# Weight sums moved into the SSD stage, and a fifth feed-forward pair begun early, in a decoder layer's kernel

## The chip, the cores and the metric

The kernel runs on one core of one Trainium2 chip. The metric is the device time of one execution in microseconds (us); for the kernel before there are three runs, of which the median counts. The profile and the trace come from one more execution, which has a time of its own. Engines are called as the profile calls them: PE (TensorE matmuls), PEld (TensorE's weight loads), DVE (VectorE), ACT (ScalarE), POOL (GpSimd), SP (SyncE, which here issues the DMAs).

## The reference

One layer of a decoder trunk on 1024 tokens and 16 meta tokens, width 1024, all in float32. What matters here:

```
proj = h @ w_in          # q_lat, kv_lat, k_pe, z, xbc, dt_raw, g_attn, g_ssd
y_attn = mla_branch(q_lat, kv_lat, k_pe, ...)        # attention over latents
y_ssd  = ssd_branch(z, xbc, dt_raw, ...)             # Mamba-2 SSD mixer, 4 groups
mixed  = sigmoid(g_attn) * y_attn + sigmoid(g_ssd) * y_ssd
h = layer_norm(DEEPNORM_ALPHA * h + mixed @ w_out)
u = causal_dwconv(h @ w_up)                          # 2 x 2816 columns, width 3
gate, val = split(u)
ffn = (silu(gate) * val) @ w_down
h = layer_norm(DEEPNORM_ALPHA * h + ffn)
```

## The kernel before

Every product in float32 is made of three passes of matmuls: each operand is split into a high part (rounded by ACT) and a low part (source minus high part, on DVE), and high times high, low times high and high times low are summed. `split` (lines 198 to 200) does it for one tile, `load_w` (143 to 164) for a weight that comes by DMA, `mm3` (166) and `mm3h` (184, matmuls at line 191) multiply.

The program has stages, which overlap a little at their borders: the first norm and the latents, attention by heads (to about 540 us of the trace), the gates stage (540 to 740), the SSD stage (740 to 1420), the output projections by two halves of the tokens with the middle norm (1420 to 1750), the feed-forward up stage (1750 to 2227), the down stage and the last norm (to 2475).

**Gates stage** (loop at 778 to 788). Eight turns m of `gate` and `o_proj` matmuls. Between them are set `dt_chain` (701: step sizes of the SSD, mostly DVE; its transposes on PE, line 736, wait for the copy of line 733), `h_centered` (751: its matmul, line 762, waits for DVE's sums of line 760) and `down_sums` (738). `down_sums(j)`, called for j = 0 to 10, loads two 512 KB blocks of the down weight, makes four differences of 128 x 512 on DVE (lines 744 to 747) and stores both blocks again; the down stage reads them 1500 us later.

**SSD stage** (loop at 867). Four groups g, in each the B and C parts and four tiles ti: a convolution (`conv`, 799), the chunk work, and the z gate, whose last DVE operation is the multiply of line 951. Each tile has two weights of 512 KB through `load_w`, which has two raw buffers. The 16 row sums `wm` of the output weight (line 1018, DVE), which the projections need, stand in the code behind this stage, but run when their buffers in pool Dr are free.

**Up stage** (line 1084 on). The up projection is a Strassen-Winograd product by halves: for each of 22 pairs f of column blocks seven products (numbers 1 to 7) of 24 matmuls instead of eight. `wload` reads the blocks, POOL makes four weight sums s1 to s4 (lines 1108 to 1111), and `wsplit` splits what the products take. The right operands ("forms") are made from the two halves of the normed tokens: B1 of the first half, T1 to T4 and B2 once the second half's norm is known. Products 1 and 2 need B1 alone. So `NHEAD` = 4 pairs are "begun": `top(f)` and `second(f)` make their products 1 and 2 while the norm's root is taken and the forms are made. In the loop (1213 to 1255) a begun pair then has five products left, a whole pair all seven. `first(f)` (1140) sets up a pair: for a begun one its product 6 into the PSUM pair x0 and the addition u2 = p1 + x0 on DVE (line 1148). Product 5 overwrites x0, so it waits for that addition.

A scheduler sets the order of the instructions on each engine from priorities and dependences; `issue_after` ties one instruction behind another. Each engine, and SP's queue of DMA issues, works in order.

Of the kernel before, what the change touches and what calls it, by code (L numbers as in the profile page):

```python
# [103 lines left out]
def tile_hybrid(ctx: ExitStack, tc: tile.TileContext, x, vecs, consts, cos, sin, win, wqb, wk, wv,  # L104
# [156 lines left out]
    gv_d = [dtile(f"gv_d{k}", [P, SEQ]) for k in range(NFF)]  # L261
    t13_d = [dtile(f"t13_d{k}", [P, D]) for k in range(KH)]
# [413 lines left out]
    with pool("B3", 1) as p3:  # L676
# [61 lines left out]
        def down_sums(j):  # L738

            x, y = (p3.tile([P, D], F32, name=k, tag=k) for k in ("tw1", "tw2"))  # L740
            nc.sync.dma_start(x, wdl[j])
            nc.sync.dma_start(y, wdl[j + KH])
            (b11, b12), (b21, b22) = ((t[:, :512], t[:, 512:]) for t in (x, y))
            nc.vector.tensor_sub(b11, b12, b11)
            nc.vector.tensor_sub(b12, b22, b12)
            nc.vector.tensor_sub(b22, b22, b11)
            nc.vector.tensor_sub(b21, b21, b22)
            nc.sync.dma_start(t13_d[j], x)
            nc.sync.dma_start(t42_d[j], y)

# [27 lines left out]
        for m in range(KT):  # L778
# [18 lines left out]
    with pool("C", 1) as p:  # L797
# [36 lines left out]
        def norm_factors(g, ssq):  # L834

            for b in range(3):
# [4 lines left out]
                nc.sync.dma_start(rr_d[g][:, lo(b):C1[b]], r[:, off:n])  # L841

        ngs = 0
        late = None
        for g in range(GROUPS):
# [21 lines left out]
            for i in range(4):  # L867
# [11 lines left out]
                for b in range(3):  # L879
# [71 lines left out]
                    nc.vector.tensor_mul(y[:, off:n], y[:, off:n], tz[:, off:n])  # L951
# [26 lines left out]
    p = eD.enter_context(pool("Dr", 1, "right"))  # L978
# [57 lines left out]
    for hi in range(2):  # L1036
# [136 lines left out]
    with tc.issue_after(root_end[0]):  # L1173
        second(0)
# [344 lines left out]
```

## Time and profile before

| what | us |
|---|---|
| runs, median (lowest to highest) | 2478.08 (2471.75 to 2480.24) |
| the profiled execution's own time | 2476.96 |
| its span in the trace | 2474.9 |
| PE busy in the span | 2379.6 (96%) |
| DVE busy | 1746.3 (71%) |
| ACT busy | 1137.5 (46%) |
| POOL busy | 202.2 (8%) |

The span is the time from the first to the last instruction of the trace. A share is an average over stages with different limits. The mean granted TensorE clock of this execution was 0.986 of full speed.

### The profile page before, as it was taken

The numbers are of one execution on the slowest core, as the hardware profiler recorded it, in microseconds if no ns is written. First come the engines' busy times: TensorE is split into PE (matmuls) and PEld (weight loads), VectorE is DVE, ScalarE is ACT, GpSimd is POOL, SyncE is SP. The second block draws the span as 40 slices with busy tenths as digits, with TensorE's granted clock in tenths as the row PEclk, the third lists the DMA queues.
The fourth block names the chain that finished last, engine by engine and source line by source line (L and its number), as shares of the span: only waits on it lengthen the run. The fifth ranks groups of instructions, "written<-read, shape, count | busy, mean of one in ns | idle before, by whom it ended". The sixth has DMA issues, their size and how long they took to land.

```text
span 2474.9 us, 42581 instructions
## 1 busy us (share of the span) xinstructions
PE 2379.6 (96%) x16319; PEld 2252.3 (91%) x16319; DVE 1746.3 (71%) x3945; ACT 1137.5 (46%) x2481; POOL 202.2 (8%) x190
## 2 busy tenths in 40 slices
PE   6999999999999999999999999999789999999996
PEld 5998988989999999999999999999789999998885
DVE  6467667676767678776877744855778777766858
ACT  5335545562226555445554432432544444445443
POOL 0000000000000000000000000202332222210004
PEclk9999999999999999999999999999899999999998
DMA  6120110147792312222212254644322222229332
GB/s 205 47 66 29 42 38 26 46 137 254 246 308 85 101 64 87 82 79 89 84 64 82 66 176 139 212 154 148 116 86 81 83 83 81 78 85 304 123 111 98
DMA packets 124620, 277.29 MB, mean 112 GB/s; under 512 B 14720, under 2 KB 49792, under 8 KB 122368
## 3 DMA queue, kind: packets, MB, share of 16 engines
q1 hardware_dynamic: 124416, 274.57, 33.8%
q8 instruction: 128, 2.10, 0.3%
q14 instruction: 76, 0.62, 0.1%
HBM read 209.62 MB, written 62.80 MB: 110 GB/s over the span
## 4 chain that ended last, share of the span: by engine, by line
PE 80%; DVE 8%; DMA 6%; issue 2%; ACT 2%; POOL 1%; SPq 0%; DVEq 0%; ACTq 0%; POOLq 0%
PE d L191 25%; PE g L171 11%; PE g L173 11%; PE g L172 11%; PE g L1339 5%; PE c L617 3%; PE c L1339 2%; PE c L908 2%; PE c L611 1%; PE c L932 1%; PE c L912 1%; DMA yl<-y_d 1%; DMA tw<-wdl 1%; DMA wraw<-wup 1%; DVE wl L161 1%
## 5 line engine op out<-in xcount | busy, mean ns | idle before, releaser
L191 PE MATMUL d<-f,wh 128*128 128x258 f32 (+1 forms) x4000 | 655.5, 286 | 28.2 <-DVE u L1148 15.7
L191 PEld LDWEIGHTS d<-f,wh 128*128 128x128 f32 x4000 | 558.7, 192 | 31.0 <-ACT wh L199 20.0
L171 PE MATMUL g<-h,wh 128*128 128x348 f32 (+3 forms) x1560 | 508.0, 326 | 4.7 <-ACT lat L399 4.7
L172 PE MATMUL g<-h,wl 128*128 128x348 f32 (+3 forms) x1560 | 507.4, 325 | 0.0
L173 PE MATMUL g<-h,wh 128*128 128x348 f32 (+3 forms) x1560 | 507.0, 325 | 0.0
L191 PE MATMUL d<-f,wl 128*128 128x258 f32 (+1 forms) x2000 | 407.6, 285 | 6.1 <-DVE wl L200 4.3
L191 PEld LDWEIGHTS d<-f,wl 128*128 128x128 f32 x2000 | 314.4, 192 | 7.9 <-DVE wl L200 5.5
L171 PEld LDWEIGHTS g<-h,wh 128*128 128x128 f32 x1560 | 295.4, 189 | 7.4 <-ACT lat L399 5.0
L172 PEld LDWEIGHTS g<-h,wl 128*128 128x128 f32 x1560 | 295.8, 190 | 2.7 <-issue 2.7
L173 PEld LDWEIGHTS g<-h,wh 128*128 128x128 f32 x1560 | 295.1, 189 | 2.7 <-issue 2.7
L161 DVE TENSOR_TENSOR wl<-wraw,wh 128x512 fp32r<-128x512 f32 (+2 forms) x278 | 193.6, 698 | 142.1 <-ACT wh L160 138.9
L160 ACT CAST wh<-wraw 128x512 fp32r<-128x512 f32 (+2 forms) x278 | 167.1, 604 | 254.8 <-PE d L191 122.6
L171 PE MATMUL g<-a,wh 128*128 128x348 f32 (+2 forms) x456 | 149.2, 328 | 1.9 <-DVE kn L200 1.1
L172 PE MATMUL g<-a,wl 128*128 128x348 f32 (+2 forms) x456 | 148.1, 325 | 0.0
L173 PE MATMUL g<-a,wh 128*128 128x348 f32 (+2 forms) x456 | 147.8, 324 | 0.0
L200 DVE TENSOR_TENSOR wl<-wraw,wh 128x512 fp32r<-128x512 f32 x136 | 99.6, 741 | 60.3 <-ACT wh L199 60.2
L199 ACT CAST wh<-wraw 128x512 fp32r<-128x512 f32 x136 | 82.7, 617 | 106.5 <-DMA wraw<-wup 48.9
L813 DVE SCALAR_TENSOR_TENSOR xc<-g,V,xc 128x347 f32<-128x347 f32 (+2 forms) x180 | 103.5, 576 | 33.0 <-ACT xc L809 30.2
L898 ACT ACTIVATE G<-ac,tok 116x116 f32<-116x116 f32 x288 | 91.6, 379 | 42.5 <-PE c L908 42.5
L1339 PE MATMUL g<-wh,dh 128*128 128x512 f32 x352 | 110.7, 396 | 0.0
L1133 DVE SCALAR_TENSOR_TENSOR va<-u,V,va 128x512 f32<-128x512 f32 x88 | 94.8, 1077 | 20.4 <-ACT va L1131 19.1
L199 ACT CAST wh<-s 128x512 fp32r<-128x512 f32 x88 | 53.9, 617 | 88.2 <-PE d L191 45.6
(306 smaller groups left out, 4216.0 us busy)
## 6 DMA issues: line engine op xcount, KB each, us to landing
wraw<-win SPq DMA_DIRECT2D x65, 512.0 KB, 3.4
wraw<-wup SPq DMA_DIRECT2D x48, 512.0 KB, 3.4
ac<-cs_d SPq DMA_DIRECT2D x16, 1044.0 KB, 5.7
wraw<-wos SPq DMA_DIRECT2D x32, 512.0 KB, 3.9
tw<-wdl SPq DMA_DIRECT2D x22, 512.0 KB, 4.6
t_d<-tw SPq DMA_DIRECT2D x22, 512.0 KB, 3.1
gv<-gv_d SPq DMA_DIRECT2D x44, 256.0 KB, 5.9
wraw<-t_d SPq DMA_DIRECT2D x44, 256.0 KB, 3.4
```

The lines of the kernel that those rows point to most:

```text
L160: nc.scalar.copy(h[:, :n * ncol], r)
L161: nc.vector.tensor_sub(l[:, :n * ncol], r, f32(h[:, :n * ncol]))
L171: nc.tensor.matmul(ps, ah, bh, start=(k == 0), stop=False)
L172: nc.tensor.matmul(ps, al, bh, start=False, stop=False)
L173: nc.tensor.matmul(ps, ah, bl, start=False, stop=(k == n - 1))
L191: ins = nc.tensor.matmul(ps[:, PO + c0:PO + c1], a, b[:, c0:c1], start=(start and k == 0 and i == 0), stop=(k == n - 1 and i == 2), skip_g ...
L199: nc.scalar.copy(H, src)
L200: nc.vector.tensor_sub(L, src, f32(H))
L813: nc.vector.scalar_tensor_tensor(t[:, l:n], ps[:, hal + l - s:hal + n - s], vec("cw", (3 - s) * 24 + ct), t[:, l:n], ALU.mult, ALU.add)
L898: nc.scalar.activation(G_[:, k * S:(k + 1) * S], ac[:S, hh, C0[b] + k * S:C0[b] + (k + 1) * S], AF.Relu, bias=tok[:, 3 * b + k, 32 + hd:33 ...
L1133: nc.vector.scalar_tensor_tensor(t, src[:, 2 - k:HN - k], vec("fw", (2 - k) * 44 + ti), t, ALU.mult, ALU.add)
L1339: nc.tensor.matmul(pss[t], a[:, o], b, start=(first and j == 0 and i == 0), stop=(j == KH - 1 and i == 2), skip_group_check=not first)
```

## The change

The sums `down_sums` leave the gates stage. They are made in the SSD stage, after the tiles ti = 1 to 11, from a pool "DS" of their own with two buffers of each kind, and their first subtraction is tied behind the last multiply of the tile. Pool Dr is divided (into `prr`, Dt and others). Five pairs are begun instead of four: the fifth, pair 4, is begun first, and its two partial results lie in DRAM until its turn. In the loop begun and whole pairs take turns: 0, 5, 4, 6, 1, 7, 2, 8, 3, 9, then 10 to 21. `prod` ties each product behind the one before it, so that PE keeps the order of the program. The norm's forms are made in the order T2, T3, T1, then `first(0)`, then B2 and T4; the four subtractions for T4 (b21) go from POOL to DVE, ahead of `first(0)`. No product is added or left out.

```diff
-            for j in range(2 * m - 2, 2 * m):
-                if 0 <= j < KH:
-                    down_sums(j)
...
+    with pool("DS", 2, "right") as pds, pool("C", 1) as p:
...
+        def down_sums(j, after):
+            x, y = (pds.tile([P, D], F32, name=k, tag=k) for k in ("tw1", "tw2"))
+            nc.sync.dma_start(x, wdl[j])
+            nc.sync.dma_start(y, wdl[j + KH])
+            (b11, b12), (b21, b22) = ((t[:, :512], t[:, 512:]) for t in (x, y))
+            with tc.issue_after(after):
+                nc.vector.tensor_sub(b11, b12, b11)
+                nc.vector.tensor_sub(b12, b22, b12)
+                nc.vector.tensor_sub(b22, b22, b11)
+                nc.vector.tensor_sub(b21, b21, b22)
+            nc.sync.dma_start(t13_d[j], x)
+            nc.sync.dma_start(t42_d[j], y)
...
-                    nc.vector.tensor_mul(y[:, off:n], y[:, off:n], tz[:, off:n])
+                    ins = nc.vector.tensor_mul(y[:, off:n], y[:, off:n], tz[:, off:n])
...
+                if 0 < ti <= KH:
+                    down_sums(ti - 1, ins.ins)
...
     def prod(ps, q, w, start=True):
-        return mm3h(ps, w[q], rhs[q], start)
+        with tc.issue_after(order[0]) if order else ExitStack():
+            ins = mm3h(ps, w[q], rhs[q], start)
+        order[:] = [ins.ins]
+        return ins
...
     def first(f):
...
-        if f < NHEAD:
+        if f < NHEAD + NMORE:
+            if f >= NHEAD:
+                for k in ("p1", "c11"):
+                    q[k] = etile(k, NHEAD)
+                    nc.sync.dma_start(q[k], hx_d[f - NHEAD][k])
             prod(q["x0"], 6, q["w"])
...
     def second(f):
...
+        if f >= NHEAD:
+            for k in ("p1", "c11"):
+                nc.sync.dma_start(hx_d[f - NHEAD][k], st[f][k])
...
+    heads = [*range(NHEAD, NHEAD + NMORE), *range(NHEAD)]
...
+    for j in range(hB):
+        b21.append(ftile(prr, F32))
+        nc.sync.dma_start(b21[j], h1_d[j + hB][:, cols(0)])
     for j in range(hB):
         T1[j] = form(pf2, b11[j])
     for j in range(hB):
+        nc.vector.tensor_sub(b21[j], b21[j], t2[j])
+    rhs.update({5: T1, 6: T2, 7: T3})
...
+    first(0)
+    for j in range(hB):
         B2[j] = form(pf2, rs[j + hB])
     for j in range(hB):
-        b21 = dtmp("b21", "r", 8)
-        nc.sync.dma_start(b21, h1_d[j + hB][:, cols(0)])
-        nc.gpsimd.tensor_sub(b21, b21, t2[j])
-        T4[j] = form(pf2, b21)
-    rhs.update({3: B2, 4: T4, 5: T1, 6: T2, 7: T3})
+        T4[j] = form(pf2, b21[j])
+    rhs.update({3: B2, 4: T4})
...
-    first(0)
-    begun = 1
-    for f in range(NFF):
+    turns = [f for pr in itertools.zip_longest([0, NHEAD, *range(1, NHEAD)], range(NHEAD + NMORE, NFF)) for f in pr
+             if f is not None]
+    for f, nxt in zip(turns, turns[1:] + [None]):
         q = st[f]
-        while begun < min(NHEAD, f + 2):
-            first(begun)
-            begun += 1
...
-        while begun < min(NFF, f + (3 if f + 1 < NHEAD else 2)):
-            first(begun)
-            begun += 1
+        if nxt:
+            first(nxt)
         prod(x0, 3, w, False)
```

**DVE, the sums of one block.** Before, they stand in the gates stage among the `dt_chain` (lines 715 to 724); tw1 and tw2 are the two blocks:

```order
L744 TENSOR_TENSOR tw1_7807<-tw1_7807 128x512
L745 TENSOR_TENSOR tw1_7807<-tw2_7808,tw1_7807 128x512
L746 TENSOR_TENSOR tw2_7808<-tw2_7808,tw1_7807 128x512
L723 TENSOR_SCALAR xx_8018<-xx_8018 64x348
L747 TENSOR_TENSOR tw2_7808<-tw2_7808 128x512
L715 TENSOR_SCALAR w_8021<-u_8020 64x348
L716 RECIPROCAL w_8021<-w_8021 64x348
L161 TENSOR_TENSOR wl_7622<-wraw_7619,wh_7621 128x512
```

Now they stand at the end of an SSD tile, here ti = 6, by turns with the next tile's convolution (line 800, tile xc):

```order
L952 TENSOR_TENSOR y_12369<-y_12369,tz_12400 128x344
L837 TENSOR_TENSOR tw1_12407<-tw1_12407 128x512
L800 SCALAR_TENSOR_TENSOR xc_12452<-g_12427,V_72,xc_12452 128x347
L959 TENSOR_TENSOR ssq_11480<-ssq_11480,tz_12400 128x344
L838 TENSOR_TENSOR tw1_12407<-tw2_12408,tw1_12407 128x512
L800 SCALAR_TENSOR_TENSOR xc_12452<-g_12427,V_72,xc_12452 128x346
L839 TENSOR_TENSOR tw2_12408<-tw2_12408,tw1_12407 128x512
L800 SCALAR_TENSOR_TENSOR xc_12452<-g_12427,V_72,xc_12452 128x345
L840 TENSOR_TENSOR tw2_12408<-tw2_12408 128x512
L804 SCALAR_TENSOR_TENSOR xc_12452<-th_12457,xc_12452 128x348
```

In the same move the 16 row sums wm went from the place between the gates and the SSD stage to group 3, behind the sums of tile ti = 11, because their buffers lie where pool DS lies.

**SP, the DMA issues at the end of the same tile.** Before, with the stores of y, the next weights (wraw) and the decay rows (ac):

```order
L952 DMA y_d6_172<-y_12261 128x334
L952 DMA y_d6_172<-y_12345 128x348
L147 DMA wraw_12940<-win 128x1024
L952 DMA y_d6_172<-y_12424 128x344
L147 DMA wraw_13086<-win 128x1024
L873 DMA ac_13574<-cs_d_188 128x2088
```

Now:

```order
L953 DMA y_d6_174<-y_12206 128x334
L953 DMA y_d6_174<-y_12290 128x348
L149 DMA wraw_12905<-win 128x1024
L953 DMA y_d6_174<-y_12369 128x344
L841 DMA t13_d5_129<-tw1_12407 128x1024
L842 DMA t42_d5_140<-tw2_12408 128x1024
L833 DMA tw1_13419<-wdl 128x1024
L834 DMA tw2_13420<-wdl 128x1024
L149 DMA wraw_13051<-win 128x1024
L874 DMA ac_13549<-cs_d_190 128x2088
```

Two stores and two loads stand ahead of the next weight load; the loads take the buffers that those of an earlier block free.

**PE, the start of the feed-forward loop.** Before, d_21039 is x0 of pair 0, wh_21027 a weight of product 6 and wh_21031 one of product 5; the last four rows of product 6 and the first four of product 5:

```order
L191 MATMUL d_21039<-f_20918,wl_21028 128x258
L191 MATMUL d_21039<-f_20918,wl_21028 128x256
L191 MATMUL d_21039<-f_20919,wh_21027 128x258
L191 MATMUL d_21039<-f_20919,wh_21027 128x256
L191 MATMUL d_21039<-f_20942,wh_21031 128x258
L191 MATMUL d_21039<-f_20942,wh_21031 128x256
L191 MATMUL d_21039<-f_20942,wl_21032 128x258
L191 MATMUL d_21039<-f_20942,wl_21032 128x256
```

Now, with d_21081 as x0, wh_21069 for product 6, and d_21144 (x2), wh_21065 for product 7:

```order
L193 MATMUL d_21081<-f_20992,wl_21070 128x258
L193 MATMUL d_21081<-f_20992,wl_21070 128x256
L193 MATMUL d_21081<-f_20993,wh_21069 128x258
L193 MATMUL d_21081<-f_20993,wh_21069 128x256
L193 MATMUL d_21144<-f_20997,wh_21065 128x258
L193 MATMUL d_21144<-f_20997,wh_21065 128x256
L193 MATMUL d_21144<-f_20997,wl_21066 128x258
L193 MATMUL d_21144<-f_20997,wl_21066 128x256
```

Product 7, into another PSUM pair, now stands between products 6 and 5.

**DVE at the same place.** Before, the low parts (line 200) of the last T1 form, of B2 (r) and T4 (b21) stand ahead of the addition u2, line 1148:

```order
L200 TENSOR_TENSOR f_20955<-f_20868,f_20954 128x514
L200 TENSOR_TENSOR f_20959<-r_20364,f_20958 128x514
L200 TENSOR_TENSOR f_20963<-r_20431,f_20962 128x514
L200 TENSOR_TENSOR f_20967<-r_20498,f_20966 128x514
L200 TENSOR_TENSOR f_20971<-r_20565,f_20970 128x514
L200 TENSOR_TENSOR f_20978<-b21_20974,f_20977 128x514
L200 TENSOR_TENSOR f_20985<-b21_20981,f_20984 128x514
L200 TENSOR_TENSOR f_20992<-b21_20988,f_20991 128x514
L200 TENSOR_TENSOR f_20999<-b21_20995,f_20998 128x514
L1148 TENSOR_TENSOR u2_21064<-p1_20618,d_21039 128x514
L200 TENSOR_TENSOR wl_21020<-wraw_21009,wh_21019 128x512
L200 TENSOR_TENSOR wl_21032<-s1_21011,wh_21031 128x512
```

Now the subtractions of line 1225 (b21), a weight of pair 5 (s3_21211), the last T1 form and one B2 form stand ahead of it (line 1164):

```order
L1225 TENSOR_TENSOR f_21018<-f_21018,t2_20964 128x514
L202 TENSOR_TENSOR f_21033<-f_20940,f_21032 128x514
L202 TENSOR_TENSOR wl_21230<-s3_21211,wh_21229 128x512
L202 TENSOR_TENSOR f_21037<-f_20942,f_21036 128x514
L1225 TENSOR_TENSOR f_21020<-f_21020,t2_20977 128x514
L1225 TENSOR_TENSOR f_21022<-f_21022,t2_20990 128x514
L202 TENSOR_TENSOR f_21109<-f_20373,f_21108 128x514
L1164 TENSOR_TENSOR u2_21106<-p1_20670,d_21081 128x514
L202 TENSOR_TENSOR wl_21074<-s1_21053,wh_21073 128x512
L202 TENSOR_TENSOR wl_21078<-s4_21056,wh_21077 128x512
L202 TENSOR_TENSOR f_21113<-f_20440,f_21112 128x514
L202 TENSOR_TENSOR f_21117<-f_20507,f_21116 128x514
```

Of the forms behind T1, three B2 forms and all of T4 now stand behind the addition. From the fourth T2 form to the addition DVE has 22 instructions in the new order.

## Rows read from the trace of the kernel before

**Rows 1.** The page's part 1: busy us, share of the span, instructions of each engine.

```profile
PE 2379.6 (96%) x16319; PEld 2252.3 (91%) x16319; DVE 1746.3 (71%) x3945; ACT 1137.5 (46%) x2481; POOL 202.2 (8%) x190
```

**Rows 2.** Windows, up stage: us, busy of PE, PEld, DVE, ACT, POOL; clock, DMA, GB/s.

```profile
1910.00:2210.00 300.00, 300.00 (x2487) 300.00 (x2486) 228.92 (x297) 146.37 (x238) 77.20 (x56) 1.00 0.25 82
1770.00:1870.00 100.00, 72.06 (x535) 69.00 (x535) 81.59 (x105) 45.49 (x73) 42.97 (x27) 0.88 0.25 82
1770.00:1800.00 30.00, 13.25 (x81) 12.10 (x80) 25.05 (x33) 18.09 (x30) 15.92 (x9) 0.66 0.25 80
1790.00:1800.00 10.00, 5.68 (x24) 5.27 (x24) 7.41 (x10) 6.24 (x9) 3.81 (x4) 0.51 0.18 53
```

**Rows 3.** Waits of PE, whole span: line, releaser, us in all, times, longest.

```profile
PE d L191 <- DVE u L1148: 15.7, 1, 15.7
...
PE c L736 <- DVE q L733: 3.6, 2, 3.4
...
PE c L762 <- DVE hs L760: 2.1, 1, 2.1
```

**Rows 4.** Timeline of PE, 1755 to 1795 us: start, length, line, tiles, shapes, count, [idle before].

```profile
1755.24 1.35 PE L227 MATMUL d<-K,ir 128*128 128x128 f32 x10
...
1777.73 0.50 PE L191 MATMUL d<-f,wh 128*128 128x258 f32 x2 [0.42 <-DVE f L200]
...
1793.97 0.77 PE L191 MATMUL d<-f,wh 128*128 128x258 f32 x2 [15.73 <-DVE u L1148]
```

**Rows 5.** Timeline of DVE, 1770 to 1795 us.

```profile
1771.15 4.08 DVE L200 TENSOR_TENSOR wl<-s,wh 128x512 fp32r<-128x512 f32 x3
...
1776.99 0.69 DVE L200 TENSOR_TENSOR f<-t,f 128x514 fp32r<-128x514 f32 x1
...
1783.63 2.50 DVE L200 TENSOR_TENSOR f<-r,f 128x514 fp32r<-128x514 f32 x4
```

**Rows 6.** Timeline of POOL, 1765 to 1795 us.

```profile
1767.26 1.50 POOL L1108 TENSOR_TENSOR s<-wraw 128x512 f32<-128x512 f32 x1 [32.95 <-DMA wraw<-wup]
...
1772.24 1.61 POOL L1111 TENSOR_TENSOR s<-wraw,s 128x512 f32<-128x512 f32 x1
1781.67 10.18 POOL L1205 TENSOR_TENSOR b<-b,t 128x514 f32<-128x514 f32 x4 [7.81 <-DMA b<-h_d]
```

**Rows 7.** The page's part 6, DMA issues: transfer, count, KB each, median us to landing.

```profile
wraw<-wup SPq DMA_DIRECT2D x48, 512.0 KB, 3.4
...
t_d<-tw SPq DMA_DIRECT2D x22, 512.0 KB, 3.1
```

**Rows 8.** Windows, gates stage, same columns as rows 2.

```profile
620.00:660.00 40.00, 36.42 (x214) 35.21 (x214) 30.78 (x62) 9.36 (x21) 0.00 (x0) 0.91 0.64 223
680.00:700.00 20.00, 20.00 (x129) 20.00 (x128) 10.11 (x20) 4.01 (x8) 0.00 (x0) 1.00 0.98 326
700.00:720.00 20.00, 17.94 (x104) 17.22 (x103) 13.46 (x27) 4.24 (x9) 0.30 (x3) 0.91 0.83 268
```

**Rows 9.** Groups of DVE, 540 to 740 us: busy, mean ns, idle before and releaser.

```profile
L1018 DVE TENSOR_REDUCE wm<-wr 128x1 f32<-128x512 f32 x12 | 7.9, 681 | 3.3 <-DMA wr<-wor 3.3
L744 DVE TENSOR_TENSOR tw<-tw 128x512 f32<-128x512 f32 x11 | 7.6, 689 | 9.0 <-DMA tw<-wdl 9.0
```

**Rows 10.** Windows, SSD stage: about one tile, and a stretch of group 3.

```profile
848.00:880.00 32.00, 31.73 (x222) 29.64 (x221) 25.81 (x65) 19.00 (x48) 0.13 (x2) 1.00 0.29 92
1240.00:1280.00 40.00, 40.00 (x270) 39.05 (x269) 28.86 (x60) 18.13 (x37) 0.10 (x1) 1.00 0.13 43
```

**Rows 11.** Timeline of SP's queue, 866 to 900 us: y stores and weight loads.

```profile
867.00 0.32 SPq L952 DMA_DIRECT2D y_d<-y  x1
875.10 0.33 SPq L147 DMA_DIRECT2D wraw<-win  x1
...
892.71 0.33 SPq L147 DMA_DIRECT2D wraw<-win  x1
898.88 0.32 SPq L952 DMA_DIRECT2D y_d<-y  x1
```

More of the change, by code (lines that the diff above doesn't have):

```diff
@@ L1 @@
+import itertools
 from contextlib import ExitStack
@@ L90 @@
 NHEAD = 4
+NMORE = 1
 KH = NFF // 2
@@ L261, in tile_hybrid @@
     gv_d = [dtile(f"gv_d{k}", [P, SEQ]) for k in range(NFF)]
+    hx_d = [{k: dtile(f"hx_{k}{j}", [P, HN]) for k in ("p1", "c11")} for j in range(NMORE)]
     t13_d = [dtile(f"t13_d{k}", [P, D]) for k in range(KH)]
@@ L737, in dt_chain @@
                 nc.scalar.copy(tok[:, 3 * c:3 * c + 3, :], tp[:S, :192].rearrange("p (a b) -> p a b", b=64))
[L738 to L749, printed above, removed]
         def h_centered(c):
@@ L796, in tile_hybrid @@
     NB = 348
-    with pool("C", 1) as p:
+    with pool("DS", 2, "right") as pds, pool("C", 1) as p:
         def conv(blk, ct, tag, bufs):
@@ L977, in tile_hybrid @@
     eD = ctx.enter_context(ExitStack())
-    p = eD.enter_context(pool("Dr", 1, "right"))
+    prr = eD.enter_context(pool("Dr", 8, "right"))
+    eT = ctx.enter_context(ExitStack())
+    p = eT.enter_context(pool("Dt", 1, "right"))
     eM = ctx.enter_context(ExitStack())
@@ L1115, in wrest @@
             for q, a in ((4, a22), (7, s3), (6, s2), (5, s1), (3, s4)):
-                r[q] = wsplit(p0, a, 4) if q in (7, 6, 3) else wsplit(pe[0], a, 3)
+                r[q] = wsplit(p0, a, 4) if q in (4, 7, 6) else wsplit(pe[0], a, 3)
             return r
+    order = []
     def prod(ps, q, w, start=True):
-        return mm3h(ps, w[q], rhs[q], start)
+        with tc.issue_after(order[0]) if order else ExitStack():
+            ins = mm3h(ps, w[q], rhs[q], start)
+        order[:] = [ins.ins]
+        return ins
     pe = []
     def etile(name, bufs):
-        return (p0 if name in ("p1", "c11") else pe[0]).tile([P, HN], F32, name=name, tag=name, bufs=bufs)
+        pl = p0 if name in ("p1", "c11") else pe[0] if name in ("u2", "u4") else pe[1]
+        return pl.tile([P, HN], F32, name=name, tag=name, bufs=bufs)
     def conv_up(src, ti, tag, bufs):
@@ L1169, in top @@
         return ins
-    rd = inv_root(ssq, HN, 1.0 / D, LN_EPS, top(0), lambda: top(1))
+    heads = [*range(NHEAD, NHEAD + NMORE), *range(NHEAD)]
+    rd = inv_root(ssq, HN, 1.0 / D, LN_EPS, top(heads[0]), lambda: top(heads[1]))
     with tc.issue_after(root_end[0]):
-        second(0)
-    second(1)
-    for f in range(2, NHEAD, 2):
-        top(f)
-        top(f + 1)
-        second(f)
-        second(f + 1)
+        second(heads[0])
+    second(heads[1])
+    for i in range(2, len(heads), 2):
+        for f in heads[i:i + 2]:
+            top(f)
+        for f in heads[i:i + 2]:
+            second(f)
     T1, T2, T3, T4, B2 = ([None] * hB for _ in range(5))
@@ L1197, in tile_hybrid @@
         T3[j] = form(pf2, rs[j])
+    b21 = []
+    for j in range(hB):
+        b21.append(ftile(prr, F32))
+        nc.sync.dma_start(b21[j], h1_d[j + hB][:, cols(0)])
     for j in range(hB):
@@ L1220, in tile_hybrid @@
         prod(x2, 7, w)
-        if f < NHEAD:
+        if f < NHEAD + NMORE:
             c11, u2 = q["c11"], q["u2"]
@@ L1233, in tile_hybrid @@
         u4 = etile("u4", 2)
-        if f < NHEAD:
+        if f < NHEAD + NMORE:
             nc.vector.tensor_add(u4, p1, half(x0))
```

16 lines of the change are left out of this document (9 added, 7 removed).

## The prediction

> **What bounds the kernel now.** I read the share of each engine first, then the waits of PE, then windows, and only for one place the timelines. PE is busy for 96% of the span and no other engine for more than 71% [rows 1]; the change neither adds nor drops a product, so it can only win back time in which PE idles or runs at the lower of its two clock levels (1.2 instead of 2.4 GHz; the profile's clock column is 1.00 at the higher). A measurement of this kernel can tell 0.3% from no change, 7.4 us.
>
> The rate to measure by: in the steady part of the up stage 2487 matmuls fill 300 us without a gap [rows 2], 0.1206 us each. A product of 24 is 2.9 us, a whole pair of seven 20.2 us, the five products of a begun pair 14.5 us.
>
> Two places lose time that the change touches. The large one is the passage into the up stage: in 1770 to 1870 PE is busy for 72.06 us of 100 [rows 2], so 27.9 us are idle, and in 1790 to 1800 the clock is 0.51, 24 matmuls take 5.68 us where the rate gives 2.9, which is 2.8 more. Loss 30.7 us. (By counts, 535 matmuls at 0.1206 are 64.5 us, loss 35.5; some records can be missing, so I keep the lower.) The reader is to see that half of it is one wait: PE sat 15.73 us until the addition u2 of line 1148 was done [rows 3, 4]. On PE product 5 of pair 0 stood directly behind product 6, whose sum that addition reads and whose PSUM product 5 overwrites. On DVE the addition stood behind the forms, and the last of these behind POOL, whose four b21 subtractions ran from 1781.67 for 10.18 us [rows 6]. What is left, 12 us of idle, is spread over four begun pairs in a row, each with few matmuls to hide its weights.
>
> The small one is the gates stage: 3.6 us of idle for the dt transposes and 2.1 for the centering matmul [rows 3], both waits for DVE, in stretches with a clock of 0.91 [rows 8].
>
> **The change part by part.** *Start of the up stage.* After the root (PE's row at 1755.24, done by 1756.6) come eight products instead of six ahead of product 6, because a fifth pair is begun: 8 x 2.9 = 23.2, to 1779.8 [rows 4]. Product 6's weights: POOL's first sum began at 1767.26, the fourth at 1772.24 [rows 6], so three sums take 5.0. In the new order one more top weight comes first; I take its split as done at about 1769.6, the load behind it 3.4 [rows 7], so 1773.0, sums to 1778.0, rounding and split about two DVE operations of 0.63 each plus lock (below) 0.8: 1780.1. PE idles 0.3 us here. Products 6 and 7 run to 1785.9.
>
> The addition u2: the fourth T2 form began at 1776.99 and ended 0.6 later, behind three weight splits that took 4.08 [rows 5]; these move behind it and one more top split, 0.6, comes ahead, so 1777.6 - 4.08 + 0.6 = 1774.1. From there DVE has 22 instructions, of which the trace has the price 2.50/4 = 0.63 each [rows 5]: 13.9. Five POOL sums (four of pair 0, one of pair 5) fall into this time. How much each slows DVE the trace bounds from both sides: the four forms at 1783.63 ran at 0.63 each while POOL subtracted, nothing lost; the three splits at 1771.15 took 4.08 instead of 1.9, with 2.7 us of POOL's work beside them, so 2.2/2.7 of POOL's time, 1.3 us a sum. I take 1.0, nearer the second, since those were sums of the same kind: 5.0. The addition ends at 1774.1 + 13.9 + 5.0 = 1793.0. PE, free at 1785.9, waits 7.1 us where it waited 15.7. I keep one product at the lower clock, +2.8, as the trace shows it after such a wait.
>
> The rule that speaks against this step is in the Trainium skill, "SBUF — State Buffer", section "SBUF: two separate sides": a VectorE operation with two SBUF inputs and a GpSimd operation that reads SBUF shut each other out for the whole instruction. Taken in full for VectorE, with a sum at 5.0/3 = 1.65 us [rows 6], five sums cost 8.3 instead of 5.0, product 5 starts 3.3 us later, and the sum below becomes 2459. The splits at 1771.15 lie near that rule; the forms at 1783.63 lost nothing, and there POOL's subtractions took 2.5 us each, as if POOL had been the one shut out.
>
> The remaining weight waits, 12 us over four begun pairs in a row, fall as whole pairs stand between them: DVE and POOL then have 34.7 us of PE for two pairs instead of 29. I take 3 us for all five (none to 12). Loss after 0.3 + 7.1 + 2.8 + 3 = 13; the gain is 30.7 - 13 = 18 (bounds 9, when the weight waits stay at 12, and 28, when the addition comes in time). The spill of pair 4, two stores and two loads of 263 KB, costs nothing: its loads are issued a whole pair (20 us) ahead of their use and a load of 512 KB lands in 3.4 [rows 7]; without that cover one load, 3.4. The b21 subtractions on DVE are 4 of the 22.
>
> *Gates stage.* Without the sums DVE sheds 44 x 0.689 = 30 us and waits for their loads (9.0 us before line 744 alone [rows 9]), which held up what was queued behind. The transposes and the centering matmul need the same DVE results with a shorter queue. Idle 5.7, and a lower clock behind it: against 129 matmuls per 20 us [rows 8], 620 to 660 has 44 fewer and 700 to 720 has 25 fewer, 69 x 0.155 = 10.7 us in all. I take 7 (bounds 3 and 10.7): the chain of dt is long on DVE even alone.
>
> *SSD stage.* Each of eleven tiles gets four subtractions, 2.74 us by line 744 [rows 9], 30 in all; a tile of 31.9 us (stores at 867.00 and 898.88 [rows 11]) has 6.2 us of idle DVE [rows 10]. They fit, but not at any moment: they stand between the next convolution's operations, which free PSUM for PE. The 16 row sums, 10.9 us, go where DVE has 11.1 us idle in 40 [rows 9, 10]. On SP two stores that wait for the sums, and two loads that wait until an older store has landed (3.1 us [rows 7]), now stand ahead of the next weight load. That load is late by some 2.7 + 3.1 = 6 us; weight loads are 17.6 us apart [rows 11] and need 3.4, so it is hidden. DMA is at 0.29 there, and 2 MB more per tile are 66 GB/s beside 92 [rows 10]; the gates stage moved 326 [rows 8]. Bounds 0 and 30.2 + 10.9 = 41, all of it on the path; I take 4, near the lower end, because PE is busy for 31.73 of 32 us there with DVE idle for a fifth.
>
> **Sum.** 2476.96 (the profiled execution, 1.1 below the median of the runs) - 18 - 7 + 4 = **2456 us**.
>
> **The rivals.**
> 1. *The addition is nearly as late* (lock in full, weight waits stay), gain 10, and the gates stage gives back 5, since dt's own chain on DVE stays: 2477 - 10 - 5 + 4 = 2466. For it: splits at 1.36 us instead of 0.63 beside POOL. Against: the long POOL subtractions are gone.
> 2. *Almost all comes back*: the addition in time, gain 28, gates 7, SSD free: 2442. For it: 6.2 us of idle DVE in each tile. Against: 22 instructions and five sums from 1774 end 7 us too late by the sum above.
> 3. *No change*: the gain at the start is 9, and of the 41 us a third, 14, comes up in the SSD stage and eats the 7 of the gates: 2475. The sums would then merely have changed their place.
> 4. *Slower*: in each SSD tile the subtractions hold up the next convolution's operations on DVE, so PSUM comes free late and PE waits: 41 against 25, 2493. It decides from 25/11 = 2.3 us a tile on, most of the 2.74. For it: the sums stand between those of line 800, and SP's weight load behind them. Against: idle DVE and the slack of that load.
> That the change doesn't do what it says is ruled out by the order: product 7 stands between 6 and 5, and the sums behind the tiles.
>
> **How the numbers follow.** Forecast 0.58, rival 1 0.18, rival 2 0.14, rivals 3 and 4 0.05 each. The first three are all below 2470.6, over 0.3% faster: 0.90. Rival 3 is the same, 0.05, rival 4 slower, 0.05. The range goes from 2438 (28 and 10.7 won, nothing paid) to 2470 (rival 1 with the SSD stage at twice its price): it leaves out rivals 3 and 4 and some of the ends.
>
> **What would show it.** In the new profile product 7 stands behind 6, and the wait of PE for line 1164 is about 7 us instead of 15.7; windows of the first 100 us of the up stage idle by 10 to 13 us; the gates stage has no waits for the dt copy and the centering sums, and a clock of 1.00; an SSD tile shows DVE at about 28.5 of 32 us, PE still at 31 or more. The forecast is wrong if the SSD tiles are longer than 31.9 us by more than 0.5, if PE waits for DVE in line 800 or SP's weight loads there, if the addition comes in time (rival 2) or as late as before (rival 1).

## The result and the profile after

The changed kernel takes 2453.02 us in the median of 4 runs (2446.29 to 2453.69), beside 2479.16 us for the kernel before in runs of the same series. The ratio is 0.9894, with a 95% interval from 0.9874 to 0.9915: faster by some 26 us. The forecast was 2456 us, its range 2438 to 2470. The profiled execution took 2452.51 us, with a span of 2450.7, 24.2 below that of before.

Its shares are almost those of [rows 1] (the page's part 1); with the same 16319 matmuls PE is busy for 4 us less:

```profile
PE 2375.2 (97%) x16319; PEld 2249.8 (92%) x16319; DVE 1741.6 (71%) x3951; ACT 1135.2 (46%) x2480; POOL 199.3 (8%) x186
```

To see where the time went, I cut both traces at the same four marks: the gate activations, the last multiply of the SSD tiles, the matmuls at the end of the second norm's root, and the first matmul of the down stage. Each row (timelines of one line each) gives the count, the duration in ns, and the first and last start. Before:

```profile
L696 ACT ACTIVATE ga<-g x24: 449/452/463, 570.6 to 727.8; 128x334 f32<-128x334 f32 x8, 128x348 f32<-128x348 f32 x8, 128x344 f32<-128x344 f32 x8
L951 DVE TENSOR_TENSOR y<-y,tz x48: 498/514/520, 776.2 to 1407.8; 128x334 f32<-128x334 f32 x16, 128x348 f32<-128x348 f32 x16, 128x344 f32<-128x344 f32 x16
L227 PE MATMUL d<-K,ir x10: 170/275/356, 1755.2 to 1756.3; 128*128 128x128 f32 x8, 128*128 128x2 f32 x2
L1339 PE MATMUL g<-wh,dh x352: 389/395/486, 2236.1 to 2422.7; 128*128 128x512 f32 x176
```

After:

```profile
L699 ACT ACTIVATE ga<-g x24: 450/454/463, 573.6 to 721.4; 128x334 f32<-128x334 f32 x8, 128x348 f32<-128x348 f32 x8, 128x344 f32<-128x344 f32 x8
L952 DVE TENSOR_TENSOR y<-y,tz x48: 499/516/520, 768.5 to 1398.0; 128x334 f32<-128x334 f32 x16, 128x348 f32<-128x348 f32 x16, 128x344 f32<-128x344 f32 x16
L229 PE MATMUL d<-K,ir x10: 170/275/356, 1744.5 to 1745.6; 128*128 128x128 f32 x8, 128*128 128x2 f32 x2
L1362 PE MATMUL g<-wh,dh x352: 387/395/502, 2211.4 to 2398.6; 128*128 128x512 f32 x176
```

The differences of these starts are the stages. The gates stage went from 157.2 to 147.8 us (-9.4), the way from the last gate to the first multiply from 48.4 to 47.1 (-1.3), the SSD stage from 631.6 to 629.5 (-2.1), the projections from 348.5 to 347.6 (-0.9), the up stage, from the last root matmul on, from 479.8 to 465.8 (-14.0). The rest is the start, 3.0 later (over all executions of this study it lies between 569.2 and 574.0, with little in the code ahead of it changed), and the end, 0.5 longer. The sum is -24.2.

The windows of the changed kernel, with the columns of [rows 2]; the rows answer to [rows 8], [rows 10] and [rows 2]:

```profile
540.00:740.00 200.00, 199.44 (x1261) 197.18 (x1260) 107.42 (x214) 67.22 (x152) 0.30 (x3) 1.00 0.48 155
840.00:872.00 32.00, 31.73 (x217) 29.61 (x215) 27.73 (x69) 18.14 (x45) 0.13 (x2) 1.00 0.48 158
1232.00:1272.00 40.00, 40.00 (x271) 39.25 (x271) 37.58 (x79) 16.67 (x36) 0.15 (x2) 1.00 0.52 175
1760.00:1860.00 100.00, 89.81 (x700) 88.43 (x699) 88.61 (x115) 51.76 (x88) 38.74 (x24) 0.95 0.32 106
1770.00:1780.00 10.00, 10.00 (x66) 10.00 (x66) 8.93 (x15) 6.28 (x13) 3.25 (x1) 0.75 0.48 159
1790.00:1800.00 10.00, 7.74 (x52) 7.77 (x53) 9.22 (x12) 5.23 (x9) 6.05 (x4) 0.83 0.17 55
1860.00:1900.00 40.00, 39.06 (x324) 38.85 (x323) 35.76 (x45) 18.85 (x31) 14.86 (x10) 1.00 0.26 87
1900.00:2200.00 300.00, 296.78 (x2452) 295.96 (x2451) 226.03 (x301) 142.99 (x230) 77.16 (x54) 1.00 0.25 80
```

The gates stage is full and at full clock. In group 3 of the SSD stage DVE is at 37.58 of 40 us, with the 16 row sums beside the subtractions, and PE has no gap. The passage into the up stage has 10.2 us of idle PE instead of 27.9. The last two rows show what the forecast had not: where the kernel before ran without a gap (40.00 of 40 us in its window 1870 to 1910, and the row of 300 us in [rows 2]), the changed one idles for 0.9 and 3.2 us.

The waits of PE (columns of [rows 3]):

```profile
PE d L193 <- DVE u L1259: 7.8, 5, 3.3
...
PE d L193 <- ACT p L1187: 3.5, 1, 3.5
...
PE d L193 <- DVE u L1164: 1.7, 1, 1.7
...
PE c L739 <- DVE q L736: 0.4, 1, 0.4
```

Three more waits of the kernel before, for comparison: for low and high parts of weights, and for its addition u4 (line 1235 there):

```profile
PE d L191 <- DVE wl L200: 4.3, 5, 1.4
PE d L191 <- ACT wh L199: 3.2, 4, 1.5
PE d L191 <- DVE u L1235: 3.0, 2, 2.2
```

Line 1164 is the addition u2, line 1259 the addition u4 of a begun pair (its product 3 overwrites what u4 reads), line 1187 the copy of p1. The wait of 15.7 us for u2 has become 1.7, and those for weights are gone, but the wait for p1 is new and that for u4 has grown from 3.0 to 7.8. The addition u2 itself comes hardly earlier: product 5, which waits for it, starts 37.7 us behind the root's last matmul before (1793.97 [rows 4], 1756.3) and 37.1 us now (1782.68, 1745.6; PE's row is shown below). The wait is shorter because PE gets there later: it has two products of pair 4 and product 7 of pair 0 more to do in that time, some 8.7 us, and waits for p1 on the way.

### The profile page after: what moved, and what is told of

Same layout as the page of the kernel before. It is cut to its first block, busy times and chain, and to the rows that moved or that the text cites. A ratio compares the mean times of both kernels' runs of the same rounds, so it can differ in the third digit from the quotient of the medians.

```text
span 2450.7 us, 42685 instructions
## 1 busy us (share of the span) xinstructions
PE 2375.2 (97%) x16319; PEld 2249.8 (92%) x16319; DVE 1741.6 (71%) x3951; ACT 1135.2 (46%) x2480; POOL 199.3 (8%) x186
## 4 chain that ended last, share of the span: by engine, by line
PE 79%; DVE 9%; DMA 4%; ACT 2%; issue 2%; POOL 1%; SPq 0%; DVEq 0%; ACTq 0%; POOLq 0%
PE d L193 20%; PE g L173 12%; PE g L175 12%; PE g L174 12%; PE g L1362 4%; PE c L620 3%; PE c L1362 2%; PE c L909 2%; PE c L933 1%; DMA yl<-y_d 1%; PE c L614 1%; PE c L913 1%; DVE wl L202 1%; DMA wraw<-wup 1%; PE c L567 1%
## 5 line engine op out<-in xcount | busy, mean ns | idle before, releaser
L193 PE MATMUL d<-f,wl 128*128 128x258 f32 x2000 | 406.2, 285 | 1.8 <-DVE wl L163 1.8
L620 PE MATMUL c<-ptt,v 116*128 116x344 f32 (+7 forms) x288 | 91.3, 436 | 1.2 <-ACT ptt L619 0.5
L577 ACT ACTIVATE p<-c,nm 115x348 f32<-115x348 f32 (+4 forms) x144 | 72.2, 503 | 42.6 <-DVE nm L575 31.5
```

Source lines behind the costliest of these rows:

```text
L193: ins = nc.tensor.matmul(ps[:, PO + c0:PO + c1], a, b[:, c0:c1], start=(start and k == 0 and i == 0), stop=(k == n - 1 and i == 2), skip_g ...
L620: nc.tensor.matmul(ops[:, o0:n], vt[j][:w, hh * P:(hh + 1) * P], ptt[:w, o0:n], start=(j == 0), stop=(j == nbmax - 1))
```

## The experiments

All profiled executions were cut at the same marks. The stages in us, and the ratio of the times to those of the kernel before with its interval:

| kernel | gates | SSD | up | ratio |
|---|---|---|---|---|
| before | 157.2 | 631.6 | 479.8 | |
| changed | 147.8 | 629.5 | 465.8 | 0.9894 (0.9874 to 0.9915) |
| sums_only | 147.8 | 629.1 | 480.4 | 0.9941 (0.9917 to 0.9965) |
| up_only | 155.8 | 631.6 | 465.8 | 0.9943 (0.9922 to 0.9965) |
| gates_no_subs | 153.0 | 631.5 | 480.6 | 0.9968 (0.9954 to 0.9982) |
| gates_no_loads | 147.8 | 630.4 | 481.0 | one run, 2466.89 us beside 2477.95 |
| ssd_double | 147.8 | 631.4 | 467.2 | 0.9906 (0.9884 to 0.9927) |
| four_begun | 147.7 | 629.9 | 471.1 | 0.9903 (0.9878 to 0.9928) |
| begun_in_row | 147.7 | 629.1 | 475.4 | 0.9909 (0.9884 to 0.9933) |
| b21_pool | 147.8 | 629.9 | 465.9 | 0.9889 (0.9859 to 0.9918) |
| no_tie | 147.7 | 629.2 | 465.0 | 0.9884 (0.9864 to 0.9905) |
| tops_chain | 147.7 | 629.6 | 468.8 | 0.9896 (0.9873 to 0.9918) |
| u_copy | 147.7 | 629.4 | 468.9 | 0.9888 (0.9865 to 0.9910) |
| chain_u_copy | 147.7 | 629.3 | 467.6 | 0.9883 (0.9860 to 0.9907) |

A stage is from one profiled execution of each kernel. The gates and SSD stages repeat well where their code is the same (gates 147.7 or 147.8 in eleven executions, SSD 629.1 to 629.9 in nine), the up stage less so: 465.8, 465.8 and 467.2 with the changed code, 479.8 to 481.0 with the code before (four executions). Differences of the up stage under some 1.5 us are therefore not told apart. The whole times repeat only within some 0.2%; so the parts are told apart by the stages.

### Each half of the change alone

`sums_only` is the kernel before with the move of the sums alone; `up_only` is the changed kernel with the sums put back:

```diff
-                if 0 < ti <= KH:
-                    down_sums(ti - 1, ins.ins)
...
+            for j in range(2 * m - 2, 2 * m):
+                if 0 <= j < KH:
+                    down_sums(j)
```

Expected of `sums_only`:

> The kernel before with the sums of the down weight moved into the SSD stage and nothing else. Theory (the sums' place is one part of the gain, the up stage another, and they add): the gates stage, first to last gate activation, falls from 157.2 us to about 148, the SSD stage stays at 630 to 632 us, the up stage, from the root to the down stage, stays at 480.8; time about 2477 - 11 = 2466. Rival (the sums' place gains nothing by itself; what came in the gates stage is due to the new placing of buffers or of the wm sums): gates stage about 156, time within 3 us of before.

Expected of `up_only`:

> The changed kernel with the sums put back into the gates stage. Theory (parts add): gates stage about 157 us, up stage about 467, time about 2477 - 14 = 2463. Rival (the parts depend on each other, the up stage gains only with the other buffers): up stage over 472, time over 2469.

Measured: gates 147.8 and up stage 480.4 for the first, gates 155.8 and up stage 465.8 for the second. Each half has its own stage's gain and leaves the other's alone, and 0.9941 x 0.9943 is 0.9884, within the interval of the whole. The parts add; both rivals fall. The 2.1 us that the SSD stage became shorter come with the sums (629.1 in the first, 631.6 in the second); what in their move brings them is not shown.

### What the sums cost in the gates stage

`gates_no_subs` leaves the subtractions out of the kernel before:

```diff
-            nc.vector.tensor_sub(b11, b12, b11)
-            nc.vector.tensor_sub(b12, b22, b12)
-            nc.vector.tensor_sub(b22, b22, b11)
-            nc.vector.tensor_sub(b21, b21, b22)
```

> The kernel before without the four subtractions of each sum; their loads and stores stay where they are (the down product then has wrong weight sums). Theory (the subtractions and their waits for loads in DVE's queue held up the dt chain and the centering): gates stage about 149 us, the waits of PE for the dt copy (3.6) and the centering sums (2.1) fall to under 1, DMA share of 540 to 740 stays near 0.8. Rival (the 23 MB of loads and stores are what costs, through weights that come late): gates stage stays at 155 to 157 us, the two waits stay.

Measured: 153.0 us, less than half of the gain. The wait of PE for the dt copy stayed, that for the centering sums went. The stage's waits of PE, its window and SP's queue at the third dt load (xx) in this kernel:

```profile
PE c L736 <- DVE q L733: 4.1, 1, 4.1
```

```profile
540.00:740.00 200.00, 195.76 (x1230) 193.89 (x1229) 114.03 (x224) 63.31 (x142) 0.31 (x3) 0.99 0.84 279
```

```profile
628.54 0.33 SPq L744 DMA_DIRECT2D t_d<-tw  x1
628.97 0.38 SPq L147 DMA_DIRECT2D wraw<-win  x1
629.44 0.72 SPq L699 DMA_DIRECT2D m_d<-ga  x1
630.22 0.47 SPq L745 DMA_DIRECT2D t_d<-tw  x1
630.74 0.50 SPq L712 DMA_DIRECT2D xx<-dt_d  x1
```

The 87 KB of dt rows are issued behind 512 KB of weights and two stores of 512 KB. The tile's own view says how long its three loads took to land, and when its first DVE operation (line 723) started:

```profile
L723 DVE TENSOR_SCALAR xx<-xx x3: 326/332/333, 566.0 to 637.1; 64x348 f32<-64x348 f32 x2, 64x344 f32<-64x344 f32 x1
...
DMA to landing us min/median/max: 4.1/4.9/5.8
```

So I took the other half away. `gates_no_loads` keeps the subtractions, on one pair of blocks loaded once:

```diff
-            x, y = (p3.tile([P, D], F32, name=k, tag=k) for k in ("tw1", "tw2"))
-            nc.sync.dma_start(x, wdl[j])
-            nc.sync.dma_start(y, wdl[j + KH])
+            if not dsx:
+                dsx.extend(p3.tile([P, D], F32, name=k, tag=k) for k in ("tw1", "tw2"))
+                nc.sync.dma_start(dsx[0], wdl[0])
+                nc.sync.dma_start(dsx[1], wdl[KH])
+            x, y = dsx
...
-            nc.sync.dma_start(t13_d[j], x)
-            nc.sync.dma_start(t42_d[j], y)
```

> The kernel before with the subtractions where they were, but on one pair of blocks that is loaded once: 20 of the 22 loads and all 22 stores of the sums leave the gates stage (blocks of the unchanged down weight are copied in the SSD stage instead, so the down product is wrong). Theory after the run without subtractions (gates stage 153.0 of 157.2 us, wait for the dt copy still 4.1): the other half is transfers in SP's queue that bring the dt rows and the weights late; gates stage 150 to 153 us, wait for the dt copy under 2, DMA share of 540 to 740 about 0.5. Rival (the two halves are one and the same delay and either alone holds it): gates stage over 155.

Measured: 147.8 us, the whole gain, with all 44 subtractions still there. Waits of PE, window and tile xx:

```profile
PE c L736 <- DVE q L733: 0.4, 1, 0.4
```

```profile
540.00:740.00 200.00, 199.49 (x1264) 197.91 (x1263) 142.92 (x275) 68.05 (x154) 0.30 (x3) 1.00 0.52 169
```

```profile
L723 DVE TENSOR_SCALAR xx<-xx x3: 325/325/331, 566.2 to 633.5; 64x348 f32<-64x348 f32 x2, 64x344 f32<-64x344 f32 x1
...
DMA to landing us min/median/max: 2.2/2.4/6.5
```

DVE is busy for 142.92 us, against 107.42 in the changed kernel, and PE has no more gaps than there. The third dt load, issued at 630.4 there and 630.7 in the run before, reaches DVE at 633.5 instead of 637.1. The transfers are the cause: on their own they cost 5.2 us (153.0 against 147.8), and another 4.2 when the subtractions are there to wait for them at the head of DVE's queue, 9.0 us before line 744 alone [rows 9]. Subtractions without late loads cost nothing. With both, in the kernel before, the third dt load is not slow but late: SP's queue issues it only at 634.9, after a wait of 3.9 us for DVE's work on the second piece, it lands in 2.3 us, and line 723 starts at 638.3. Loads and stores were taken away together, so their shares are not told apart, nor whether the place in the queue or the load on the DMA engines made the dt rows land late.

### How much room an SSD tile has

`ssd_double` makes each tile's four subtractions twice:

```diff
                 nc.vector.tensor_sub(b21, b21, b22)
+                nc.vector.tensor_sub(b11, b12, b11)
+                nc.vector.tensor_sub(b12, b22, b12)
+                nc.vector.tensor_sub(b22, b22, b11)
+                nc.vector.tensor_sub(b21, b21, b22)
```

> The changed kernel with the subtractions in the SSD tiles doubled, 8 instead of 4 in each of eleven tiles (the sums then come out wrong). Theory (DVE has 6 us idle in a tile of 32, and operations queued behind 2.7 us of subtractions are early enough): the stage, first to last y multiply, goes from 629.5 to 630 to 640, time 0 to 10 us over the changed kernel. Rival (the first four only just fit, each further one is on the path): plus 30 us, stage about 660.

Measured: the stage 631.4 us, 1.9 more, for 44 more subtractions, 30 us by their own durations. Its window and its waits of PE for DVE in the stage:

```profile
764.00:1396.00 632.00, 629.86 (x4344) 593.14 (x4343) 523.97 (x1321) 330.54 (x795) 1.83 (x20) 1.00 0.36 120
```

```profile
PE g L173 <- DVE xc L800: 1.4, 4, 0.8
```

The first sign of PE waiting for the convolution on DVE appears here, 1.4 us in all, and not with the change's own four.

### What the up stage owes to which edit

`four_begun` begins four pairs, which also makes their number even:

```diff
-NMORE = 1
+NMORE = 0
...
-    turns = [f for pr in itertools.zip_longest([0, NHEAD, *range(1, NHEAD)], range(NHEAD + NMORE, NFF)) for f in pr
+    turns = [f for pr in itertools.zip_longest([*range(NHEAD)], range(NHEAD + NMORE, NFF)) for f in pr
```

> The changed kernel with four begun pairs instead of five (heads 0, 1, 2, 3; turns 0, 4, 1, 5, 2, 6, 3, 7, 8 and on). Theory (DVE's queue, not PE, sets when product 5 of pair 0 may start, so two products less ahead of it only lengthen the wait; but with an even number the 3.5 us wait for the copy of p1 in the last pair goes): up stage, from the last matmul of the root to the down stage, 465.8 now, becomes 466 to 470. Rival (the fifth pair is what fills the gap): 471 to 474.

Measured: 471.1 us, 5.3 more; the rival's figure. The two products that the changed kernel has more ahead of product 5 (5.8 us of PE) are worth nearly their length. The waits of PE from 1735 to 1990 us:

```profile
PE d L193 <- DVE u L1164: 5.1, 1, 5.1
PE d L193 <- DVE u L1259: 3.8, 4, 1.9
PE d L193 <- ACT f L201: 3.1, 2, 2.8
```

The wait for p1 is gone as expected, but u2 takes 5.1, and PE now also waits for ScalarE's part of the forms. `begun_in_row` makes the begun pairs one after the other:

```diff
-    turns = [f for pr in itertools.zip_longest([0, NHEAD, *range(1, NHEAD)], range(NHEAD + NMORE, NFF)) for f in pr
-             if f is not None]
+    turns = [0, NHEAD, *range(1, NHEAD), *range(NHEAD + NMORE, NFF)]
```

> The changed kernel with the five begun pairs one after the other (turns 0, 4, 1, 2, 3, 5, 6 and on). Theory (whole pairs between them hide the begun pairs' weights): waits for weight splits and their casts come back as before, 7 to 12 us, up stage 473 to 478 instead of 465.8. Rival (the weight waits went by the other changes, earlier forms above all): 465 to 468.

Measured: 475.4 us, 9.6 more, in the theory's range, but not by its mechanism. The waits of PE:

```profile
PE d L193 <- DVE u L1164: 7.4, 2, 6.9
PE d L193 <- DVE u L1258: 5.8, 1, 5.8
PE d L193 <- ACT p L1187: 3.6, 1, 3.6
PE d L193 <- DVE wl L202: 1.6, 3, 0.7
```

Only 2.1 us are waits for weights (with 0.5 for ScalarE's rounding). What grew most is the wait for u2, from 1.7 to 7.4; that for u4 is shorter than in the changed kernel, 5.8 instead of 7.8. The granted clock is also lower, 0.91 from 14.4 to 154.4 us behind the root's last matmul, where the changed kernel has 0.95 and then 1.00. That whole pairs between begun ones give DVE time for the additions u2 agrees with this; no run shows it by itself.

`b21_pool` gives the four subtractions back to GpSimd:

```diff
-        nc.vector.tensor_sub(b21[j], b21[j], t2[j])
+        nc.gpsimd.tensor_sub(b21[j], b21[j], t2[j])
```

> The changed kernel with the four b21 subtractions back on GpSimd, in the new place. Theory (the buffer of u2 lies where the operand of these subtractions lay, and GpSimd needs 2.5 us for each and has the weight sums besides): the addition u2 comes 4 to 10 us later, up stage 470 to 476 instead of 465.8. Rival (VectorE's queue gets shorter by four instructions of 0.6 us, which counts more): 463 to 466.

Measured: 465.9 us, no difference, in the rival's range. But the theory's step came true as well: u2 is done 2.7 us later (39.6 us behind the root's last matmul, against 36.9), and PE waits longer for it; what makes up for it is a shorter wait for u4 (7.8 in the changed kernel):

```profile
PE d L193 <- DVE u L1164: 5.5, 1, 5.5
...
PE d L193 <- DVE u L1259: 3.3, 4, 1.8
```

DVE has four instructions less, but while POOL subtracts, four forms take 6.53 us instead of 2.50 [rows 5]. Timelines of DVE and of POOL in that kernel:

```profile
1770.62 6.53 DVE L202 TENSOR_TENSOR f<-f 128x514 fp32r<-128x514 f32 x4 [0.29 <-ACT f L201]
```

```profile
1771.44 6.83 POOL L1225 TENSOR_TENSOR f<-f,t 128x514 f32<-128x514 f32 x4
```

Four forms and four subtractions fill the same 6.5 to 6.8 us, 1.0 us more for each form: what leaves DVE comes back as its wait. That is one of each in 1.7 us, where one after the other would be 0.63 and 1.28, some 1.9 (an estimate; 1.28 is the shortest sum of 128x512 on POOL in this stretch, line 1114 at 1781.22). The rule of the Trainium skill, "SBUF — State Buffer", section "SBUF: two separate sides", is that a VectorE operation with two SBUF inputs and a GpSimd operation that reads SBUF shut each other out for a whole instruction. These two rows agree with it nearly, but for some 0.2 us of each pair.

`no_tie` takes the tie from `prod`:

```diff
-        with tc.issue_after(order[0]) if order else ExitStack():
-            ins = mm3h(ps, w[q], rhs[q], start)
-        order[:] = [ins.ins]
-        return ins
+        return mm3h(ps, w[q], rhs[q], start)
```

> The changed kernel without the tie between products. In its order on PE the matmuls of the last begun pair's product 2 and of products 6 and 7 of pair 0 are then mixed, and product 5 still stands behind them; later pairs keep the same order. Theory (the order of the forms and first(0) ahead of B2 and T4 did what was needed, the tie adds nothing): the 3.5 us wait for the copy of p1 is filled, up stage 461 to 466 us instead of 465.8. Rival (the tie is what keeps product 5 from standing in front of ready work): over 470.

Measured: 465.0 us, in the theory's range and not told apart from the changed kernel. The tie adds nothing here. Which of the other edits does what was needed is shown for two of them, the fifth pair (5.3 us) and the turns (9.6), which together are already the 14.0 if they add; no run puts the old order of the forms or the old place of `first(0)` back, so their share stays open.

### Trying to win the new waits

The first edit, `tops_chain`, lets product 1 of the next begun pair stand between products 1 and 2 of each; the second, `u_copy`, copies u2 and u4 on ScalarE first; `chain_u_copy` has both:

```diff
-    second(heads[1])
-    for i in range(2, len(heads), 2):
-        for f in heads[i:i + 2]:
-            top(f)
-        for f in heads[i:i + 2]:
-            second(f)
+    for a, b in zip(heads[1:], heads[2:]):
+        top(b)
+        second(a)
+    second(heads[-1])
...
-            nc.vector.tensor_add(q["u2"], q["p1"], half(q["x0"]))
+            nc.scalar.copy(q["u2"], half(q["x0"]))
+            nc.vector.tensor_add(q["u2"], q["u2"], q["p1"])
```

Expected of `tops_chain`:

> The changed kernel with the begun pairs' first products in another order: product 1 of the next pair always stands between products 1 and 2 of a pair, so product 2 of the last pair no longer follows its own product 1 directly. Theory (VectorE's queue sets when product 5 may start): the 3.5 us wait for the copy of p1 goes, the wait for the addition u2 grows by 3 to 5 us, up stage 463 to 466 us. Rival (PE's own waits add up): the whole wait and the slower clock behind it are won, 459 to 462.

Expected of `u_copy`:

> The changed kernel with u2 and u4 of the begun pairs first copied from PSUM by ScalarE and then added to on VectorE, so that products 5 and 3 wait for a copy and not for an addition in VectorE's queue. Theory (the waits of 1.7 and 7.8 us are VectorE's queue, ScalarE has room): both fall to under 3 together, up stage 459 to 463 us instead of 465.8. Rival (ScalarE's roundings stand in the same order as VectorE's splits, so the copy comes as late): 465 to 468.

Expected of `chain_u_copy`:

> Both of the two edits before (product 1 of the next pair between a pair's first two, and the copies on ScalarE). Theory (each takes away the bound that hides the other's gain): up stage 454 to 460 us, more than the sum of the two alone. Rival (the forms for product 5 on VectorE are late next): 461 to 465.

Measured: 468.8, 468.9 and 467.6 us. All three are misses: `tops_chain` and `chain_u_copy` came out above both of their figures, `u_copy` a little over its rival's, and none is measurably faster than the change in its time. `tops_chain` removed the wait for p1, and there PE waits 6.4 us for u2 instead of 1.7. `u_copy` halved the waits for u2 and u4 (1.0 and 3.7 us, for the copies, instead of 1.7 and 7.8), but PE then waits 3.6 us for the addition behind the copy of u4 (line 1262). The time came back elsewhere. The waits of PE with both:

```profile
PE d L193 <- ACT u L1164: 5.7, 1, 5.7
PE d L193 <- DVE u L1260: 3.9, 4, 1.8
```

The copy of u2, on an engine with room, is waited for as the addition was. Timelines of DVE and of ACT in this run:

```profile
1776.64 0.69 DVE L1224 TENSOR_TENSOR f<-f,t 128x514 f32<-128x514 f32 x1
```

```profile
1777.36 0.59 ACT L1164 COPY u<-d 128x514 f32<-128x514 f32 x1
```

The copy starts 0.03 us after DVE's last b21 subtraction ends, and so it does in `u_copy` (1777.49 behind 1777.46). By the code the buffer of u2 lies where t2, an operand of these subtractions, lay, as the expectation of `b21_pool` says. The cast ahead of the copy on ACT had itself waited 0.49 us for DVE. The edit took u2 out of DVE's queue, but not out of the wait for DVE; no run gives u2 a buffer of its own.

The first 40 us after the root in the changed kernel (columns of [rows 2]):

```profile
1745.60:1785.60 40.00, 34.79 (x265) 34.20 (x264) 37.53 (x54) 25.17 (x45) 11.88 (x6) 0.91 0.45 152
```

DVE is busy for 37.5 of 40 us, for 37.2 with both edits, and for 37.3 in the kernel before, too. u2 (the addition, or the copy) is done 35.9 to 37.5 us behind the root's last matmul in every one of these kernels whose b21 subtractions are on DVE, and in the kernel before at 37.5. That DVE is the bound of this stretch agrees with that, but no run made its work there shorter (in `b21_pool` it has 48 instructions instead of 54 there, but is busy for 38.6), so it is an argument and not shown.

## Why the prediction was right

**The start of the up stage** was right in its sum and wrong in its parts. Loss in the first 100 us: forecast 13, measured 10.2 of idle and, by the rate of 0.1206 us, 2.0 and 1.5 at the lower clock (66 matmuls in 10.00 us and 52 in 7.74), 13.7. The addition u2 was to end at 1793.0 on the old scale; the root came 10.7 us earlier, which makes 1782.3. Timeline of DVE after:

```profile
1765.04 1.77 DVE L202 TENSOR_TENSOR f<-f 128x514 fp32r<-128x514 f32 x1
...
1781.85 0.68 DVE L1164 TENSOR_TENSOR u<-p,d 128x514 f32<-128x514 f32 x1
```

It ended at 1782.5. The price of a POOL sum to DVE, taken as 1.0 us, is 1.1 in the first row (1.77 against 0.63). (The four POOL subtractions of [rows 6] did not take 2.5 us each, as read there: the first took 5.59, while DVE ran the forms at 1783.63 without loss, the others 1.26 to 1.71.) But PE did not wait 7.1 us for it. Timeline of PE:

```profile
1769.64 0.80 PE L193 MATMUL d<-f,wh 128*128 128x258 f32 x2 [3.48 <-ACT p L1187]
...
1782.68 0.47 PE L193 MATMUL d<-f,wh 128*128 128x258 f32 x2 [1.69 <-DVE u L1164]
```

With five pairs taken by twos the last one stands alone: its product 2 follows its own product 1 and waits 3.48 us for the copy of p1, and the clock is at 0.75 in the window that follows. I counted eight products as one run and didn't look at how the fifth was paired. So PE was free at 1781.0 and not at 1775.2 (the forecast 1785.9, less 10.7). The wait lay ahead of the same addition, so that product 5 began when forecast; `tops_chain`, where this wait is gone and the one for u2 is 6.4, shows it. The prediction took an addition in time as the sign of rival 2. The short wait looks like that sign and isn't: the addition came as late as forecast, and PE later.

**The failed term** is the remaining waits of the begun pairs, 3 us for all five. The waits for weights, which it meant, did go, from 4.3 and 3.2 us to none in the list; but the waits for the addition u4 grew from 3.0 to 7.8 us (line 1259), and the 0.9 and 3.2 us of idle from 1860 on lie beyond the window I summed over. So this stage gave 14.0 us and not 18.

**The gates stage** gave 9.4 and 1.3 us, 10.7 in all; the forecast was 7, with 10.7 as the bound by counts. The reason was half wrong: the step "sheds 30 us and waits for their loads" put the load on DVE's queue, and the waits for the loads were the part of it that counts. The 30 us of subtractions alone cost nothing; the transfers do, through DVE's queue and through the dt rows that come late.

**The SSD stage** was to cost 4 us and cost none; the stage became 2.1 us shorter. Of the bounds, 0 and 41, the row of an idle fifth of DVE spoke for the lower. SP's queue, too, was no cost, as worked out: no wait of PE for weights appears in the stage.

The three errors, 4 too much gain in the one stage, 4 and 6 too little in the others, cancel in part and leave 5.8 us more gain than forecast (26.8 against 21 over these stages). Of these, 2.6 are taken back by the start, the projections and the end, which the forecast had at nothing (+3.0, -0.9, +0.5). That 2452.5 lies within 4 us of 2456 is thus partly luck: the gain of each stage was off by 4 to 6 us. The other cases are out: the stage of the tiles became longer than before in no run, and doubling its added work cost 1.9 us, so the rival that ends slower was far away.

## What to carry to other kernels

Work that is needed late belongs where an engine idles beside a saturated one, but ask of it first what its transfers stand in front of: here the arithmetic without its transfers was free in both places, and the loads and stores around a small urgent load were the cost. When one wait is removed, follow the same engine's next instructions: here the wait for u2 went and the one for u4 grew, and three further edits only moved the wait. When an operation goes to another engine, ask whose work still holds its buffer. Sum a passage until the rate is steady again, not over the window where the loss was.

## What the runs showed of the hardware

A load of 87 KB behind weights and stores in the same queue landed in 4.1 to 5.8 us (median of three 4.9), and with those gone in a median of 2.4 us (2.2 to 6.5, the longest being the first, issued at 558.7), at a DMA share of 0.84 and 0.52 in the stage. In a window that read 0.84 there was thus no free capacity for this urgent load.

VectorE and GpSimd at the same time gave little more than one after the other: four forms of 0.63 us took 6.53 beside four subtractions that took 6.83. And 44 more subtractions of 0.69 us in a stage of 630 us, in which PE is busy for all but 2 us, cost 1.9 us.
